# A hybrid decoder layer on one core: the prompts' scores as plain fp32 matmuls of two key heads side by side, in four visits for eight

## The chip, the cores and the metric

The kernel runs on one core of a Trainium2 chip. The metric is the device time of one execution in microseconds; for the kernel before it is 1594.37 us, the median of 3 runs (1593.99 to 1594.84). One further execution was profiled; all views of the trace are of that one.

## The reference

One decoder layer for 256 prompt tokens and 64 sample tokens (8 sequences of 8) that share the weights, model width 2048. What matters here is the attention of the prompt: 16 query heads in 4 groups, one key head of 64 features for each group, a window of 128 positions in blocks of 128 queries.

```python
xn = rms_norm(x, g_mix)
z = xn @ w_in                      # [B | C | h | q | k | v | gate_conv | gate_attn]
s = einsum('...qhgd,...shd->...hgqs', q, k) * HEAD_DIM ** -0.5
s = where(valid, s + bias, -inf)   # bias: a learned value by head and distance
p = exp(s - m) / (sum(exp(s - m)) + exp(sink - m))
o = einsum('...hgqs,...shd->...qhgd', p, v)
m = sigmoid(gate_c) * y_conv + sigmoid(gate_a) * (o @ w_attn_out)
h = x + m @ w_o
h = h + (silu(hn @ w_gate) * (hn @ w_up)) @ w_down     # hn = rms_norm(h, g_ffn)
```

The output is the norm of h, with new keys, values and convolution states.

## The kernel before

Features lie on partitions and all 320 tokens on the free axis. Every large product (`product`, L162 to L185) works on 256 output features: its weights come in tiles of 4 x 128 rows (`wraw`), which ScalarE (ACT) rounds to `whi` (L129) and VectorE (DVE) turns into the rest `wlo` (L130), both of type fp32r. One tile gives 24 matmuls of 320 columns (L176): each weight block three times, high by high, high by the input's low part, low by high. Sixteen input blocks make 4 tiles, so a product of this kind has 96 matmuls. `wraw` has 4 buffers, `whi` and `wlo` 3 each, so the splits may run three tiles ahead of TensorE (PE).

Behind each tile `product` calls `tick` (L144), which runs one step of a generator in `side_work`: the small work of attention is cut into such steps and laid between the tiles. Instructions are then put in order on each engine by a scheduler; `after` holds a step's work behind the last split and the last matmul. `pending` (L181) holds work that is done once behind the first tile of the following product.

The products come in this order: kv (L371), four pairs of q (`q`, heads' queries), then four rounds of C, H and B for the convolution, then the gates (`gc`, `ga`) with the convolution's and the attention's output (`yc`, `ya`), then `wo`, `fg`, `fu` and `dn`. During q the side work is `kv_work` (L784): the first norm, whose sum over partitions is two matmuls `prb` (L199), the turning of keys and values, and `keys_twice`. During the rounds of C, H and B it is `attention`: scores and softmax of the prompt, its values (`po`, L612), and the sample's attention (`pss`, L684, and `spo`, L748), the last three in plain fp32.

The scores before use the split form too. `keys_twice` (L773) writes `k2`: for each of the 4 key heads a tile of 128 rows, in which 64 rows hold the rounded keys and 64 the rest, in both orders. `q_out` (L805) scales a pair of query blocks (L808) and writes for each head pair two tiles `q2` of 128 rows, rounded queries on one half and the rest on the other (L812 on ACT, L813 on DVE); they lie in `at_t`, which takes the attention's result later. A unit is one key head and two of its four query heads; there are 8. For each unit `prompt_scores` (L537) issues 6 matmuls of 256 columns: for each of two heads two that add up for the second block of queries (L548) and one for the first block, which sees only its own 128 keys, both parts side by side (L551). `ps1` and `ps0` take a PSUM bank each, from a pool of 4 (`aux`). DVE then adds the bias, read backwards (L556, L559), takes the larger of the two halves for the second block (L557), and adds the second part for the first block (L560). `prompt_softmax`, `prompt_norm` and `prompt_turn` follow, each in a later step. `bias_load` (L527) is a transfer that POOL (GpSimd) issues, into one of two buffers.

A nudge (L193) is a single matmul of `xh` by `xl`, with contiguous columns, into an `aux` bank that nobody reads. There are four of them in the kernel before: in the kv product, twice in the sample's attention, and one of 128 columns in the first `fu` product.

The lines in question:

Of the kernel before, what the change touches and what calls it, by code (L numbers as in the profile page):

```python
# [8 lines left out]
F32 = mybir.dt.float32  # L9
F32R = mybir.dt.float32r  # L10
AF = mybir.ActivationFunctionType
# [5 lines left out]
TP, NB, TS = 256, 8, 8  # L17
T = TP + NB * TS
DC = 1024
NH, NKV, HD, GRP = 16, 4, 64, 4  # L20
DKV = NKV * HD
WIN = 128
# [5 lines left out]
P = 128  # L28
# [19 lines left out]
LEAD_X, LEAD_C, LEAD_A, LEAD_M, LEAD_F, LEAD_L = 16, 8, 8, 24, 40, 48  # L48
# [4 lines left out]
def hybrid_layer(ctx: ExitStack, tc: tile.TileContext, a: dict, o: list):  # L53
    nc = tc.nc
# [17 lines left out]
    def ps_aux(name):  # L72
        return aux[0].tile([P, 512], F32, tag="aux", name=name)
# [3 lines left out]
    def u(s):  # L77
        uid[0] += 1
        return f"{s}_{uid[0]}"
# [10 lines left out]
    def tmp(tag, name):  # L90
        return wk.tile([P, UL], F32, tag=tag, name=u(name))
# [101 lines left out]
    def nudge(rows, weights, n):  # L193
        x, w = (bass.AP(r.tensor, r.offset, [list(r.ap[0]), [1, m]]) for r, m in ((rows(0), n), (weights(0), P)))
        nc.tensor.matmul(ps_aux(u("nudge"))[:, :n], w, x, start=True, stop=True)
# [5 lines left out]
    def flip(ap):  # L201

        *rest, (step, n) = ap.ap
        return bass.AP(ap.tensor, ap.offset + (n - 1) * step, [*rest, (-step, n)])
# [15 lines left out]
    rbq = cst.tile([P, T], F32, name="rbq")  # L220
# [31 lines left out]
    xh, xl = row_tiles(xp, ("xh_t", "xl_t"), KC, LEAD_X, ("xh", "xl"))  # L252
# [21 lines left out]
    kT = zz.tile([P, 2, T], F32, name="kT")  # L274
# [188 lines left out]
    at_row = 2 * NS * JS + JS  # L463
    at_t = yy.tile([P, LEAD_A + 8 * at_row + 16], F32R, name="at_t")
# [7 lines left out]
    pr = pr_p.enter_context(tc.tile_pool(name="pr", bufs=1, side="right"))  # L472

    k2 = pr.tile([P, NKV, 2, TP], F32R, name="k2")
    k2h, k2l = k2[:, :, 0], k2[:, :, 1]

    def q2(ch, par):
        o = LEAD_A + ch * at_row + par * TP  # L480
        return at_t[:, o:o + TP]


    def kv_turn(t):

# [41 lines left out]
    def bias_load(kv, gp):  # L527
        bias = pr.tile([P, 2, 2 * WIN], F32, tag="bias", name=u("bias"), bufs=2)
        nc.gpsimd.dma_start(
            bias,  # L530
            bass.AP(
                e_scr.tensor, e_scr.offset + (kv * GRP + gp * 2) * EL, [[1, P], [EL, 2], [1, 2 * WIN]]
            ),
        )
        return bias

    def prompt_scores(kv, gp, bias):  # L537

        j, par = kv // 2, kv % 2
        s = pr.tile([P, 4, WIN], F32, tag="s", name=u("s"), bufs=3)
        ps1, ps0 = ps_aux(u("ps1")), ps_aux(u("ps0"))
        for gi in range(2):
            q = q2(j * 4 + gp * 2 + gi, par)
            for i in range(2):
                nc.tensor.matmul(  # L548
                    ps1[:, gi * 256:(gi + 1) * 256], q[:, WIN:2 * WIN], k2[:, kv, i], start=i == 0, stop=i == 1
                )  # L550
            nc.tensor.matmul(  # L551
                ps0[:, gi * 256:(gi + 1) * 256].rearrange("p (two k) -> p two k", two=2), q[:, 0:WIN],
                k2[:, kv, :, 0:WIN], start=True, stop=True,
            )
        w = pr.tile([P, 2, 2 * WIN], F32, tag="w", name=u("w"), bufs=1)
        nc.vector.tensor_add(w, ps1.rearrange("p (g k) -> p g k", g=2), flip(bias))  # L556
        nc.vector.tensor_max(s[:, 2:4], w[:, :, 0:WIN], w[:, :, WIN:2 * WIN])  # L557
        p0 = ps0.rearrange("p (g two k) -> p g two k", g=2, two=2)
        nc.vector.tensor_add(s[:, 0:2], p0[:, :, 0], flip(bias[:, :, 0:WIN]))  # L559
        nc.vector.tensor_add(s[:, 0:2], p0[:, :, 1], s[:, 0:2])  # L560
        return s

    def prompt_softmax(kv, gp, s):
        h0 = kv * GRP + gp * 2
        mx = wk.tile([P, 2, 2], F32, tag="mx", name=u("mx"))
        den = wk.tile([P, 2, 2], F32, tag="den", name=u("den"))
        es = wk.tile([P, 2, 2], F32, tag="es", name=u("es"))
        nc.vector.tensor_reduce(mx.rearrange("p b g -> p (b g)"), s, axis=AX.X, op=ALU.max)
        nc.vector.scalar_tensor_tensor(
            mx, mx, -1.0, nsink[:, h0:h0 + 2].unsqueeze(1).to_broadcast([P, 2, 2]),  # L570
            op0=ALU.mult, op1=ALU.min,
        )
        nc.vector.tensor_add(es, sink_bc[:, h0:h0 + 2].unsqueeze(1).to_broadcast([P, 2, 2]), mx)
        for n in range(4):
            b, g = n // 2, n % 2
            nc.scalar.activation(
                s[:, n], s[:, n], AF.Exp, bias=mx[:, b, g:g + 1], accum_out=den[:, b, g:g + 1]
            )
        nc.scalar.activation(es, es, AF.Exp)
        return den, es  # L580
# [44 lines left out]
    units = [(j * 2 + par, gp) for j in range(2) for gp in range(2) for par in range(2)]  # L625

    def prompt_weights(scrs):
        bias, sc, sm = {}, {}, {}
        bias[0] = bias_load(*units[0])
        for i in range(len(units) + 1):  # L630
            if i < len(units):
                if i + 1 < len(units):
                    bias[i + 1] = bias_load(*units[i + 1])
                sc[i] = prompt_scores(*units[i], bias.pop(i))
                yield
                sm[i] = prompt_softmax(*units[i], sc[i])
            yield
            if i >= 1:
                prompt_norm(sc[i - 1], *sm.pop(i - 1))
                scrs.append(prompt_turn(sc.pop(i - 1)))  # L640
# [129 lines left out]
                        nc.gpsimd.tensor_copy(dst, src.bitcast(F32))  # L770
            yield

    def keys_twice():  # L773
        for kv in range(NKV):
            j, r0 = kv // 2, kv % 2 * 64
            src = kT[r0:r0 + 64, j, 0:TP]
            for o0 in (r0, 64 - r0):
                nc.scalar.activation(k2h[o0:o0 + 64, kv, :], src, AF.Copy)
            for o0 in (r0, 64 - r0):
                nc.vector.tensor_sub(k2l[o0:o0 + 64, kv, :], src, k2h[r0:r0 + 64, kv, :].bitcast(F32))  # L780
            yield

    def kv_work():
        yield from first_norm()  # L784
        rows = []
        for t in range(3):
            rows.append(kv_turn(t))
            yield
        yield from keys_twice()
        for t in range(3):  # L790
            kv_natural(t, rows[t])
            yield
# [11 lines left out]
    def q_out(j, gp, ps):  # L804
        for c in range(2):  # L805
            g = gp * 2 + c
            t = tmp("ta", "qt")[:, :TP]
            nc.vector.tensor_mul(t, ps[c][:, :TP], rbq[:, :TP])  # L808
            for par in range(2):
                r0, o0 = par * 64, 64 - par * 64  # L810
                q = q2(j * 4 + g, par)
                nc.scalar.activation(q[r0:r0 + 64], t[r0:r0 + 64], AF.Copy)  # L812
                nc.vector.tensor_sub(q[o0:o0 + 64], t[r0:r0 + 64], q[r0:r0 + 64].bitcast(F32))  # L813
            nc.vector.tensor_mul(
                qs[:, j, :, g * TS:(g + 1) * TS], ps[c][:, TP:T].rearrange("p (b t) -> p b t", b=NB),
                rbq[:, TP:T].rearrange("p (b t) -> p b t", b=NB),
            )

    side_work[0] = kv_work()
    for j in range(2):  # L820
        for gp in range(2):
            ps = in_pair(O_Q + (j * 2 + gp) * CW, "q")
# [4 lines left out]
    for cp in range(4):  # L827
        c_sb = []
        ps = in_pair(O_C + cp * CW, "C")
        for c in range(2):  # L830
            t = tmp("ta", "csb")
            nc.vector.tensor_mul(t[:, :T], ps[c][:, :T], rbsq)
            c_sb.append(t)
        ps = in_pair(O_H + cp * CW, "H")
        conv = []
        for c in range(2):
            ch = cp * 2 + c
# [12 lines left out]
            n = UL - 2  # L850
# [10 lines left out]
        ps = in_pair(O_B + cp * CW, "B")  # L861
        for c in range(2):
            ch = cp * 2 + c
            cv, cs = conv[c]
            t = tmp("td", "bc")
# [23 lines left out]
    for mp in range(8):  # L889
        c0 = mp * CW  # L890
        sg = {}
        for nm, off, tag in (("gc", O_GC, "ta"), ("ga", O_GA, "tb")):
            ps = in_pair(off + c0, nm)
            for c in range(2):
                t = tmp(tag, nm)[:, :T]
# [3 lines left out]
        ps = product(  # L899
            lambda k0, n: load_cols(w_co, k0, n, c0), 8,  # L900
            cv_h, cv_l, "yc",
        )
        for c in range(2):
            nc.vector.tensor_mul(sg["gc", c], ps[c][:, :T], sg["gc", c])
        ps = product(
            lambda k0, n: load_cols(w_ao, k0, n, c0), 8, at_h, at_l, "ya",
        )
        for c in range(2):
            t = sg["ga", c]
# [10 lines left out]
    for mp in range(8):  # L920
        c0 = mp * CW
        ps = product(
            lambda k0, n: load_cols(w_o, k0, n, c0), KC,
            m_h, m_l, "wo",
        )
        for c in range(2):
            k = mp * 2 + c
# [8 lines left out]
            else:  # L936
                t = tmp("tc", "sq")[:, :T]
# [126 lines left out]
    for half in range(2):  # L1064
# [7 lines left out]
        for fpair in range(nf // 2):  # L1072
# [11 lines left out]
            for c in range(2):  # L1084
                t, t2 = tmp("ta", "gs")[:, :T], tmp("tb", "sg")[:, :T]
# [94 lines left out]
    ps = [ps_acc(u("dn")) for _ in range(4)]  # L1180
    sets = [(k, k + 1) for k in range(0, nf, 2)]
    sets[-2:] = [sets[-2] + sets[-1]]
    for i, ks in enumerate(sets):
# [4 lines left out]
        for k, c, m in passes(order, end):  # L1188
            cs = slice(c * P, (c + 1) * P)
            if m == 0:  # L1190
                nc.tensor.matmul(
                    turns(placed(ps[c])[:, :, JR:]), held[k][0][:, cs], turns(a_move(k)[:, :, JR:]),
                    start=k == 0, stop=k == nf - 1,
                )
            elif m == 2:
                last["mm"] = nc.tensor.matmul(
                    turns(placed(ps[c])[:, :, 0:JT]), held[k][1][:, cs], turns(a_move(k)[:, :, 0:JT]),
                    start=False, stop=k == nf - 1, skip_group_check=True,
# [4 lines left out]
    s3, h3, v, s, r = (op.tile([P, 1], F32, name=n) for n in ("s3", "h3", "vf", "sf", "rr"))  # L1203
# [4 lines left out]
    for c in range(4):  # L1208
        k = E0 // P + c
# [11 lines left out]
    for c in (2, 3):  # L1221
        k = E0 // P + c
        first, _ = h_parts(k)
# [114 lines left out]
```

## Time and profile before

| | |
|---|---|
| median of 3 runs | 1594.37 us |
| the profiled execution | 1594.48 us |
| its span, first to last instruction | 1592.8 us |
| mean granted TensorE clock | 0.998 |
| the 8 visits of the scores | 90.6 to 143.3 us |
| PE, DVE, ACT busy from 98 to 113 us | 15.00, 14.29, 8.32 of 15.00 us |
| PE, DVE, ACT busy from 113 to 128 us | 15.00, 14.87, 8.08 of 15.00 us |

The span is what the profiler saw between the first and the last instruction, 1.7 us less than the execution's own time. PE are the matmuls; PEld are the loads of weights, which run beside them. Busy times of matmuls overlap, since they are pipelined: 301 ns is the length of one of 320 columns, while the next starts after some 140 ns. The chain of work that ended last gives start, length and what, so that a run of equal matmuls divided by their count is the pace. In groups of instructions, the numbers behind the bar are busy us, mean ns of one, then the idle time before them and what ended it. In a table by stretches the columns are PE, PEld, DVE, ACT and POOL, each with its number of instructions, then the granted clock, the DMA share and GB/s.

### The profile page before, as it was taken

The page shows a single profiled execution, that of the slowest core. Times are in us where ns is not written, and L with a number is a line of the kernel's source. Part 1 is how long each engine was busy: PE and PEld are TensorE (multiplying, and loading weights), DVE is VectorE, ACT ScalarE, POOL GpSimd, SP SyncE. Part 2 cuts the span into 40 slices and gives each one's busy share as a digit, 9 for nine tenths or more (in the row PEclk, how much of TensorE's full clock was granted, in tenths as well). Part 3 has the DMA queues.
Part 4 walks back from the last instruction along what each step waited for, and adds up shares of the span by engine and source line. Part 5 has one row for each costly group of instructions (what it writes and reads, how often), then busy time and mean ns, then how long its engine had stood idle before and what let it go on. Part 6 is the DMA issues. An engine that isn't in the chain of part 4 may idle for free.

```text
span 1592.8 us, 27120 instructions
## 1 busy us (share of the span) xinstructions
PE 1584.2 (99%) x11296; PEld 1569.0 (99%) x11296; DVE 882.6 (55%) x1258; ACT 650.2 (41%) x901; POOL 125.3 (8%) x214
## 2 busy tenths in 40 slices
PE   9999999999999999999999999999999999999998
PEld 9999999999999999999999999999999999999887
DVE  7889765455444455565555555553444455555556
ACT  7555344333333333444333333333333343344443
POOL 2223342000000003320000000000000000000000
PEclk9999999999999999999999999999999999999999
DMA  8666666444444444444444444455555544445652
GB/s 274 205 188 194 214 188 217 156 156 158 159 159 154 157 157 156 159 159 156 156 155 157 159 159 159 155 153 158 158 159 159 159 155 156 155 158 159 185 173 93
DMA packets 77090, 264.51 MB, mean 166 GB/s; under 512 B 9576, under 2 KB 13000, under 8 KB 76840
## 3 DMA queue, kind: packets, MB, share of 16 engines
q1 hardware_dynamic: 71880, 249.86, 49.3%
q0 software_dynamic: 4656, 12.25, 2.5%
q8 instruction: 88, 1.44, 0.4%
q10 hardware_dynamic: 432, 0.69, 0.1%
q14 instruction: 34, 0.28, 0.1%
HBM read 256.46 MB, written 8.26 MB: 166 GB/s over the span
## 4 chain that ended last, share of the span: by engine, by line
PE 99%; ACT 0%; DVE 0%; DVEq 0%; issue 0%
PE fu L176 19%; PE fg L176 19%; PE dn L1015 12%; PE wo L176 7%; PE ga L176 7%; PE gc L176 7%; PE q L176 3%; PE B L176 3%; PE H L176 3%; PE C L176 3%; PE ya L176 3%; PE yc L176 3%; PE dn L1040 3%; PE dn L1048 2%; PE kv L371 2%; PE dl L1044 1%
## 5 line engine op out<-in xcount | busy, mean ns | idle before, releaser
L130 DVE TENSOR_TENSOR wlo<-wraw,whi 128x1024 fp32r<-128x1024 f32 (+1 forms) x460 | 562.4, 1223 | 580.1 <-ACT whi L129 569.4
L129 ACT ACTIVATE whi<-wraw 128x1024 fp32r<-128x1024 f32 (+1 forms) x460 | 485.1, 1056 | 713.0 <-PE fu L176 131.9
L176 PE MATMUL fu<-hh_t,whi 128*128 128x320 f32 x704 | 205.1, 301 | 0.0
L176 PE MATMUL fu<-hl_t,whi 128*128 128x320 f32 x704 | 205.0, 301 | 0.0
L176 PE MATMUL fg<-hh_t,whi 128*128 128x320 f32 x704 | 205.0, 301 | 0.0
L176 PE MATMUL fg<-hl_t,whi 128*128 128x320 f32 x704 | 205.0, 301 | 0.0
L1015 PE MATMUL dn<-a_t,whi 128*128 128x320 f32 x896 | 162.6, 301 | 0.0
L176 PE MATMUL fu<-hh_t,wlo 128*128 128x320 f32 x704 | 158.8, 301 | 0.0
L176 PE MATMUL fg<-hh_t,wlo 128*128 128x320 f32 x704 | 158.8, 301 | 0.0
L1015 PEld LDWEIGHTS dn<-a_t,whi 128*128 128x128 f32 x896 | 137.5, 187 | 0.0
L176 PEld LDWEIGHTS fu<-hl_t,whi 128*128 128x128 f32 x704 | 131.7, 187 | 0.0
L176 PEld LDWEIGHTS fu<-hh_t,whi 128*128 128x128 f32 x704 | 131.6, 187 | 0.0
L176 PEld LDWEIGHTS fg<-hh_t,whi 128*128 128x128 f32 x704 | 131.6, 187 | 0.0
L176 PEld LDWEIGHTS fg<-hl_t,whi 128*128 128x128 f32 x704 | 131.6, 187 | 0.0
L176 PEld LDWEIGHTS fu<-hh_t,wlo 128*128 128x128 f32 x704 | 116.1, 187 | 0.0
L176 PEld LDWEIGHTS fg<-hh_t,wlo 128*128 128x128 f32 x704 | 116.1, 187 | 0.0
L1015 PE MATMUL dn<-a_t,wlo 128*128 128x320 f32 x448 | 103.9, 301 | 0.0
L1015 PEld LDWEIGHTS dn<-a_t,wlo 128*128 128x128 f32 x448 | 74.8, 187 | 0.0
L176 PE MATMUL gc<-xh_t,whi 128*128 128x320 f32 x256 | 74.5, 301 | 0.0
L176 PE MATMUL gc<-xl_t,whi 128*128 128x320 f32 x256 | 74.5, 301 | 0.0
L176 PE MATMUL ga<-xh_t,whi 128*128 128x320 f32 x256 | 74.5, 301 | 0.0
L176 PE MATMUL ga<-xl_t,whi 128*128 128x320 f32 x256 | 74.5, 301 | 0.0
(319 smaller groups left out, 2811.0 us busy)
## 6 DMA issues: line engine op xcount, KB each, us to landing
wraw<-in_w_in_dram SPq DMA_DIRECT2D x128, 512.0 KB, 3.7
wraw<-in_w_gate_dram SPq DMA_DIRECT2D x88, 512.0 KB, 3.6
wraw<-in_w_up_dram SPq DMA_DIRECT2D x88, 512.0 KB, 3.6
wraw<-in_w_down_dram SPq DMA_DIRECT2D x88, 512.0 KB, 3.6
wraw<-in_w_o_dram SPq DMA_DIRECT2D x32, 512.0 KB, 3.6
wraw<-in_w_conv_out_dram SPq DMA_DIRECT2D x16, 512.0 KB, 3.7
wraw<-in_w_attn_out_dram SPq DMA_DIRECT2D x16, 512.0 KB, 3.7
wraw<-in_w_kv_dram SPq DMA_DIRECT2D x6, 512.0 KB, 7.7
```

What stands on the lines that cost most here:

```text
L129: last["hi"] = nc.scalar.activation(hi, src, AF.Copy)
L130: last["lo"] = nc.vector.tensor_sub(lo, src, hi.bitcast(F32))
L176: last["mm"] = nc.tensor.matmul(turns(fives(ps[c][:, :T])), w[:, k, c * P:(c + 1) * P], turns(x(kc)), start=(kc == 0 and i == 0), stop=(kc ...
L371: last["mm"] = nc.tensor.matmul(turns(fives(ps[c][:, :T])), w[:, k, c * P:(c + 1) * P], turns(x(kc)), start=(kc == 0 and m == 0), stop=(kc ...
L1015: last["mm"] = nc.tensor.matmul(turns(fives(ps[c][:, :T])), parts[k][w][:, c * P:(c + 1) * P], turns(x(k)), start=k == 0 and m == 0, stop= ...
L1040: nc.tensor.matmul(turns(placed(ps[c])), parts[k][0][:, cs], turns(a_move(k)), start=k == 0, stop=False)
L1044: nc.tensor.matmul(low, a_low(k), parts[k][0], start=k == 0, stop=k == nf - 1)
L1048: last["mm"] = nc.tensor.matmul(turns(placed(ps[c])[:, :, 0:JT]), parts[k][1][:, cs], turns(a_move(k)[:, :, 0:JT]), start=False, stop=k == ...
```

## The change

The queries stay as they are, in one fp32 tile `qf` of 8 blocks, written by the one multiplication that scales them; `q2`, `k2` and `keys_twice` are gone, and with them 24 copies on ACT and 24 subtractions on DVE. The four steps of `keys_twice` stay as empty steps, with a nudge in the second.

A visit now serves two units, the two key heads that lie on rows 0 to 63 and 64 to 127 of a block of `kT`. For each of two query heads and each of two blocks of queries it issues two matmuls, one for each half of the rows: 64 rows of queries as weights, 128 or 256 columns of keys. There are 8 matmuls in a visit and 4 visits; each takes all 4 `aux` banks. The biased scores of the two units are made in the steps where they were made before (`prompt_biased`), with one addition less each. Two bias tiles are loaded ahead, and each further one after the addition that frees its buffer. A second nudge stands in the step behind the last visit.

```diff
-    k2 = pr.tile([P, NKV, 2, TP], F32R, name="k2")
-    k2h, k2l = k2[:, :, 0], k2[:, :, 1]
-
-    def q2(ch, par):
-        o = LEAD_A + ch * at_row + par * TP
-        return at_t[:, o:o + TP]
+    qf = pr.tile([P, 8, TP], F32, name="qf")
...
-    def prompt_scores(kv, gp, bias):
-        j, par = kv // 2, kv % 2
+    def prompt_scores(j, gp):
+        both = [(ps_aux(u("ps1")), ps_aux(u("ps0"))) for _ in range(2)]
+        for gi in range(2):
+            q = qf[:, j * 4 + gp * 2 + gi]
+            for b, n in ((0, WIN), (1, 2 * WIN)):
+                for par, (ps1, ps0) in enumerate(both):
+                    rows = slice(par * 64, par * 64 + 64)
+                    nc.tensor.matmul(
+                        (ps1 if b else ps0)[:, gi * n:(gi + 1) * n], q[rows, b * WIN:(b + 1) * WIN],
+                        kT[rows, j, 0:n], start=True, stop=True,
+                    )
+        return both
+
+    def prompt_biased(ps1, ps0, bias):
         s = pr.tile([P, 4, WIN], F32, tag="s", name=u("s"), bufs=3)
-        ps1, ps0 = ps_aux(u("ps1")), ps_aux(u("ps0"))
-        for gi in range(2):
-            q = q2(j * 4 + gp * 2 + gi, par)
-            for i in range(2):
-                nc.tensor.matmul(
-                    ps1[:, gi * 256:(gi + 1) * 256], q[:, WIN:2 * WIN], k2[:, kv, i], start=i == 0, stop=i == 1
-                )
-            nc.tensor.matmul(
-                ps0[:, gi * 256:(gi + 1) * 256].rearrange("p (two k) -> p two k", two=2), q[:, 0:WIN],
-                k2[:, kv, :, 0:WIN], start=True, stop=True,
-            )
         w = pr.tile([P, 2, 2 * WIN], F32, tag="w", name=u("w"), bufs=1)
         nc.vector.tensor_add(w, ps1.rearrange("p (g k) -> p g k", g=2), flip(bias))
         nc.vector.tensor_max(s[:, 2:4], w[:, :, 0:WIN], w[:, :, WIN:2 * WIN])
-        p0 = ps0.rearrange("p (g two k) -> p g two k", g=2, two=2)
-        nc.vector.tensor_add(s[:, 0:2], p0[:, :, 0], flip(bias[:, :, 0:WIN]))
-        nc.vector.tensor_add(s[:, 0:2], p0[:, :, 1], s[:, 0:2])
+        nc.vector.tensor_add(
+            s[:, 0:2], ps0[:, 0:2 * WIN].rearrange("p (g k) -> p g k", g=2), flip(bias[:, :, 0:WIN])
+        )
         return s
...
     def prompt_weights(scrs):
-        bias, sc, sm = {}, {}, {}
-        bias[0] = bias_load(*units[0])
+        bias, both, sc, sm = {}, {}, {}, {}
+        for i in range(2):
+            bias[i] = bias_load(*units[i])
         for i in range(len(units) + 1):
             if i < len(units):
-                if i + 1 < len(units):
-                    bias[i + 1] = bias_load(*units[i + 1])
-                sc[i] = prompt_scores(*units[i], bias.pop(i))
+                if i % 2 == 0:
+                    both[i], both[i + 1] = prompt_scores(units[i][0] // 2, units[i][1])
+                sc[i] = prompt_biased(*both.pop(i), bias.pop(i))
+                if i + 2 < len(units):
+                    bias[i + 2] = bias_load(*units[i + 2])
                 yield
+                if i == len(units) - 2:
+                    nudge(xh, xl, T)
                 sm[i] = prompt_softmax(*units[i], sc[i])
             yield
...
-        yield from keys_twice()
+        for i in range(4):
+            if i == 1:
+                nudge(xh, xl, T)
+            yield
...
-            t = tmp("ta", "qt")[:, :TP]
-            nc.vector.tensor_mul(t, ps[c][:, :TP], rbq[:, :TP])
-            for par in range(2):
-                r0, o0 = par * 64, 64 - par * 64
-                q = q2(j * 4 + g, par)
-                nc.scalar.activation(q[r0:r0 + 64], t[r0:r0 + 64], AF.Copy)
-                nc.vector.tensor_sub(q[o0:o0 + 64], t[r0:r0 + 64], q[r0:r0 + 64].bitcast(F32))
+            nc.vector.tensor_mul(qf[:, j * 4 + g], ps[c][:, :TP], rbq[:, :TP])
```

More of the change, by code (lines that the diff above doesn't have):

```diff
@@ L771, in sample_attention @@
             yield
[L773 to L781, printed above, removed]
     def kv_work():
```

## The prediction, made before the changed kernel ran

> **What bounds it now.** I read the page's engine totals first, then who makes PE wait, then the chain of work that ended last, in the two stretches that hold plain fp32 work or the scores.
>
> ```profile
> span 1592.8 us, 27120 instructions
> PE 1584.2 (99%) x11296; PEld 1569.0 (99%) x11296; DVE 882.6 (55%) x1258; ACT 650.2 (41%) x901; POOL 125.3 (8%) x214
> ```
>
> ```profile
> PE wm L304 <- PEq L1321: 0.8, 1, 0.8
> ```
>
> PE is busy 1584.2 of 1592.8 us, and the only wait that the list has for it is one of 0.8 us at the very start. So the time is the sum of what PE does; other engines count only where they would make it wait. The second view is the chain from the first normalization to the first visit of the scores (start, length, what).
>
> ```profile
> 39.27 0.29 PE prb L199 x2
> 39.55 47.79 PE q L176 x336
> 87.34 3.41 PE C L176 x24
> 90.75 0.24 PE ps L548 x2
> 90.99 0.12 PE ps L551
> 91.11 0.23 PE ps L548 x2
> 91.34 0.12 PE ps L551
> ```
>
> Two things are to be seen. A visit of the scores, six matmuls of 256 columns, takes 0.24 + 0.12 + 0.23 + 0.12 = 0.71 us, or 0.118 each. And the 336 matmuls of q take 47.79 / 336 = 0.1422 us each, the 24 of C behind them 3.41 / 24 = 0.1421. The third view is the chain further on, around the three places that already use plain fp32 (po, pss, spo) and two nudges.
>
> ```profile
> 197.25 5.33 PE po L612 x48
> 202.58 3.58 PE H L176 x24
> 206.16 10.08 PE B L176 x72
> 216.24 1.99 PE pss L684 x64
> 218.23 3.62 PE B L176 x24
> 221.85 0.14 PE nudge L195
> 221.99 13.45 PE C L176 x96
> ...
> 252.24 1.92 PE spo L748 x128
> 254.16 3.58 PE B L176 x24
> 257.75 0.15 PE nudge L195
> ```
>
> Here 96 matmuls of C take 13.45, 0.1401 each: the same matmul runs at two paces, 0.1422 and 0.1400, a difference of 0.0022. The slow pace holds from prb at 39 us to the first visit of the scores. It comes back after pss, where the 24 matmuls of B take 3.62, and goes with the nudge at 221.85.
>
> **The change part by part.** The first place is PE's order at the first visit; ps are the scores' sums, k is k2, at_t holds the split queries. Before:
>
> ```order
> L548 MATMUL ps_134_1188<-k_496,at_t 128x256 x2
> L551 MATMUL ps_135_1189<-k_496,at_t 128x256
> L548 MATMUL ps_134_1188<-k_496,at_t 128x256 x2
> L551 MATMUL ps_135_1189<-k_496,at_t 128x256
> L176 MATMUL C_1137<-xh_t,whi_1203 128x16x5x4
> ```
>
> Now, at the same place, with keys and queries as they are:
>
> ```order
> L539 MATMUL ps_127_1134<-kT,qf 128x128
> L539 MATMUL ps_129_1136<-kT,qf 128x128
> L539 MATMUL ps_126_1133<-kT,qf 128x256
> L539 MATMUL ps_128_1135<-kT,qf 128x256
> L539 MATMUL ps_127_1134<-kT,qf 128x128
> L539 MATMUL ps_129_1136<-kT,qf 128x128
> L539 MATMUL ps_126_1133<-kT,qf 128x256
> L539 MATMUL ps_128_1135<-kT,qf 128x256
> L176 MATMUL C_1093<-xh_t,whi_1154 128x16x5x4
> ```
>
> Eight visits of six matmuls become four of eight: four pairs, each pair one head on rows 0 to 63 and one on rows 64 to 127. The removed work is 8 x 0.71 = 5.68 us of PE. For the new work the nearest rows are the plain fp32 ones:
>
> ```profile
> L612 PE MATMUL po<-pT,vn x32: 379/379/430, 197.2 to 202.2; 128*64 128x256 f32 x32
> L684 PE MATMUL pss<-kf,qs x64: 276/276/300, 216.2 to 218.0; 64*32 64x136 f32 x64
> ```
>
> The program issues 24 matmuls at L612 and the page has 48 records, 32 at L684 and 64 records: two records for each. The records overlap: 48 of 379 ns lie in 5.33 us, 64 of 276 ns in 1.99. At L612 two neighbours share the array by columns; at L684 four do, two by rows and two by columns. So po is 24 groups of 256 columns, pss 16 groups of 136, spo (128 records, four side by side) 32 groups of 64. What each costs, with what it does to the 24 matmuls behind it, is its length plus theirs less 24 x 0.140 = 3.36: po 5.33 + 3.58 - 3.36 = 5.55, pss 1.99 + 3.62 - 3.36 = 2.25 (of which 24 x 0.0022 = 0.05 is slow pace, so 2.20), spo 1.92 + 3.58 - 3.36 = 2.14. Two of these give a price by column and a fixed one: (5.55 - 2.20) / (24 x 256 - 16 x 136) = 0.000844 us a column, and 5.55 - 6144 x 0.000844 = 0.36 us for going in and out. They give spo 2048 x 0.000844 + 0.36 = 2.09, where it took 2.14. A visit of the change, if its pairs run side by side, is 2 x 2 groups of 128 and 2 x 2 of 256 columns: 1536 x 0.000844 + 0.36 = 1.66 us. Four are 6.64, and the scores cost 6.64 - 5.68 = 0.96 us more. No row shows two tiles of 64 rows that both use all 128 columns. The bounds are the streaming with no fixed price, 4 x 1.30 - 5.68 = -0.48, and pairs one behind the other (the second rival, below); I take side by side, since L684 is the nearest row and half of its overlap is by rows. The Trainium skill, page "TensorEngine Tiling (Array Packing)", section "Tiling Modes", lists 64x128 as two tiles that operate independently; no run here shows that form.
>
> Two nudges of 320 columns are added. The rows of today's have 0.14 and 0.15, and C behind the first is 0.01 over: 0.16 each, 0.32 together.
>
> The first new nudge stands in the q products:
>
> ```order
> L176 MATMUL q_829<-xh_t,wlo_833 128x16x5x4
> L176 MATMUL q_828<-xh_t,wlo_833 128x16x5x4
> L176 MATMUL q_829<-xh_t,wlo_833 128x16x5x4
> L195 MATMUL nudge_864<-xh_t,xl_t 128x320
> L176 MATMUL q_828<-xh_t,whi_868 128x16x5x4
> ```
>
> It comes 168 matmuls behind prb, with 192 of the 360 slow ones still to run until the first visit. If it works as the one at 221.85 did, they gain 192 x 0.0022 = 0.43. The visits themselves are another matter: the old ones ended the slow pace. Of the fp32 blocks the one on 64 rows (pss) left the slow pace; the one on 128 rows (po) left the fast one, since the 72 of B that come 24 matmuls behind it took 10.08, 0.140 each; behind spo a nudge comes too soon to tell. I take pss, being nearest: three gaps of 96 matmuls between visits, and 24 up to the second nudge, 312 x 0.0022 = 0.70. The other end is 0.
>
> What leaves the other engines is free of charge:
>
> ```profile
> L813 DVE TENSOR_TENSOR at_t<-qt,at_t 64x256 fp32r<-64x256 f32 x16 | 6.7, 420 | 1.1 <-ACT at_t L812 0.7
> ...
> L780 DVE TENSOR_TENSOR k<-kT,k 64x256 fp32r<-64x256 f32 x8 | 3.3, 418 | 0.1
> L560 DVE TENSOR_TENSOR s<-ps,s 128x256 f32<-128x256 f32 x8 | 3.3, 416 | 0.0
> ```
>
> ```profile
> L812 ACT ACTIVATE at_t<-qt 64x256 fp32r<-64x256 f32 x16 | 6.6, 415 | 6.2 <-DVE qt L808 6.0
> ```
>
> DVE loses 6.7 + 3.3 + 3.3 = 13.3 us and ACT the copies that feed these, but PE waits for neither now, so nothing of it shortens the span.
>
> What moves on DVE is the order. Before, the six operations of one unit stood between two weight splits (L556 to L573). Now two units' worth stand there, behind the first visit; s, w, mx and es are the tiles of the biased scores and their maxima:
>
> ```order
> L548 TENSOR_TENSOR w_1224<-ps_128_1135,bias_1131 128x512
> L561 SCALAR_TENSOR_TENSOR mx_1182<-mx_1182,nsink 128x4
> L549 TENSOR_TENSOR s_1223<-w_1224 128x256
> L565 TENSOR_TENSOR es_1184<-sink_bc,mx_1182 128x4
> L560 TENSOR_REDUCE mx_1260<-s_1223 128x4
> L561 SCALAR_TENSOR_TENSOR mx_1260<-mx_1260,nsink 128x4
> L565 TENSOR_TENSOR es_1262<-sink_bc,mx_1260 128x4
> L130 TENSOR_TENSOR wlo_1280<-wraw_1277,whi_1279 128x1024
> ```
>
> The split behind them, wlo_1280, belongs to the fourth product tile after the visit.
>
> ```profile
> 92.50 0.68 DVE L556 TENSOR_TENSOR w<-ps,bias 128x512 f32<-128x512 f32 x1
> ...
> 95.44 1.23 DVE L130 TENSOR_TENSOR wlo<-wraw,whi 128x1024 fp32r<-128x1024 f32 x1
> ```
>
> ```profile
> 128.00:151.00 23.00, 23.00 (x169) 23.00 (x168) 22.35 (x58) 11.98 (x35) 9.50 (x17) 1.00 0.67 202
> ```
>
> One unit took 95.44 - 92.50 = 2.94; without the second addition 2.5, two 5.0, with the split 6.2. The tile's first use of it is three tiles of 3.36 and 8 matmuls later, 11.2 us after the visit: 5.0 us to spare if DVE is up to date. DVE was busy 22.35 of 23 us late in this stretch (fourth column), and two additions less in every 15 us are 0.83, so it gets slacker, not tighter. I book 0. On POOL the loads of bias tiles, which wait for the addition two units back as before, are re-sorted among the stores of p_scr, with the convolution's copies queued behind; only DVE's later work waits for these, and PE has no wait there today.
>
> The sum: 0.96 + 0.32 - 0.43 + 0.70 = +1.55 us. The profiled execution took 1594.48 us, 0.11 above the median of the runs, 1594.37; so 1596.0 for it, and 1595.9 for a median. If the visits leave the fast pace it is 1595.2; with no fixed price as well, 0.32 - 0.43 - 0.48 = -0.59, 1593.8. A measurement of this kernel can tell about 0.2%, 3.2 us, from no change; all of these lie within that.
>
> **The rivals.** The first: the weights' loads are not hidden, since a pair needs two loads of 128 columns for each pass. A price is in the short nudge:
>
> ```profile
> 711.86 0.06 PE nudge L195
> 711.92 10.14 PE fu L176 x72
> ```
>
> A matmul of 128 columns takes 0.06, and the 72 behind it 10.14 - 72 x 0.140 = 0.06 more: 0.12 together, where streaming would be half, so about 0.12 is what a load takes when nothing covers it; the scores' 0.118 for 256 columns says the same. If the two loads of a pair go one behind the other, each of 8 passes lasts at least 0.236: a visit 8 x 0.236 + 0.36 = 2.25, four 9.00, +3.32 for the scores, and with the other terms +3.91: 1598.3, slower by 0.24%. For it: nothing in the trace loads 128 columns for two row halves. Against: spo has four loads of 32 columns in 1.92 / 32 = 0.06, which is less than one load of 128 took. There is a stronger form, that a load waits for its own half's matmul: then a 256-column pass is 0.118 + 0.216 and a 128-column one 0.118 + 0.108, a visit 4 x 0.334 + 4 x 0.226 + 0.36 = 2.60, and the whole +5.3, 1599.7. The Trainium skill, "TensorE: Matmul & The Clock Gate", section "Part 3: Packing small matmuls", says that loads overlap matmuls in flight only when the row group differs. The trace speaks against that: 96 matmuls on the same 128 rows, each with a load, run at 0.140.
>
> The second: the halves do not run side by side at all. Sixteen passes, 8 of 0.216 and 8 of 0.118, and 0.36: 3.03 a visit, 12.1 for four, +6.4, with the other terms +7.0: 1601.4, slower by 0.44%. It decides if the array takes two tiles together only where their columns differ, as in po and spo; against it is pss, whose four neighbours have two row halves.
>
> The third, also slower: DVE's double burst makes PE wait at the fourth tile after a visit. It decides if DVE comes to a visit more than 5.0 us late; then up to the burst's growth, 2.5 us, is lost at each of the three later visits, 7.5 in all: 1603.4. The busy share says no.
>
> That the change gains over 0.2% would need more than half of the 5.68 us of scores to vanish, which no row offers.
>
> **How the numbers follow.** Side by side with loads hidden, either pace: 0.80, all within 0.2%. Loads exposed: 0.08 (its weak form 0.06, its strong one 0.02). Halves in turn: 0.06. DVE's burst: 0.04. Gain: 0.02. The three cases before the gain are slower by over 0.2%, 0.18 in sum. The time is that of the likeliest case, 1595.9. The range reaches down to 1593.4 (1593.8 and half a microsecond of scatter, as the three runs of before lie 0.85 apart) and up to 1598.5, which takes in the weak form of the first rival.
>
> **What would show it.** In the changed kernel's chain: visits of about 1.66 us at four places (2.25, 2.60 or 3.03 for the rivals); a short group of q after a nudge near 63 us, then q at 0.140; the 96 matmuls between visits at 13.6 (slow) or 13.44 plus the way out; no PE wait between 90 and 155 us. I would be wrong if visits took over 2 us, if a wait of PE for wlo appeared, or if the slow pace outlived the second nudge.

## The result and the profile after

The changed kernel took 1596.91 us (median of 22 runs, 1595.96 to 1597.66), the kernel before beside it 1594.22 (median of 22; one of these runs took 4207 us, and the ratio leaves it out). The ratio is 1.0016, 95% interval 1.0010 to 1.0022: slower by 1.6 to 3.5 us, which is about the 0.2% that I had called the bound of no change. Forecast were 1595.9 us and a place between 1593.4 and 1598.5. So sign and range held, and 1.0 us of the size was missing. The profiled execution took 1597.15 us, 2.67 more than the profiled one before. First its totals:

```profile
span 1595.4 us, 27101 instructions
PE 1587.1 (99%) x11314; PEld 1569.5 (98%) x11314; DVE 871.0 (55%) x1226; ACT 640.3 (40%) x877; POOL 124.1 (8%) x214
```

PE is busy for 2.9 us more, DVE for 11.6 us and ACT for 9.9 us less. The span grew by 2.6 us, so the relief of DVE and ACT bought nothing, as expected. Where the 2.6 us lie shows in the chain that ended last (start, length, what), from the first normalization's sum to the tile behind pss:

```profile
39.24 0.29 PE prb L199 x2
39.53 23.89 PE q L176 x168
63.42 0.15 PE nudge L195
63.56 23.52 PE q L176 x168
...
90.44 1.51 PE ps L539 x16
91.95 10.28 PE C L176 x72
...
105.59 1.51 PE ps L539 x16
107.10 10.30 PE H L176 x72
...
137.45 3.58 PE C L176 x24
141.03 0.34 PE nudge L195
141.38 6.72 PE C L176 x48
148.10 14.00 PE H L176 x96
162.09 13.65 PE B L176 x96
...
199.64 5.33 PE po L604 x48
...
218.83 1.99 PE pss L681 x64
220.82 3.58 PE B L176 x24
```

In the chain before, the matmuls behind a visit and from 147 us on lost nothing (48 x 0.140 = 6.72, 96 x 0.140 = 13.44):

```profile
91.45 6.72 PE C L176 x48
...
146.85 13.44 PE H L176 x96
160.29 13.44 PE B L176 x96
```

Four things are to be read from the chain after, each as a length against a count times 0.140.

- **Visits.** One takes 1.51 us, and the 72 matmuls behind it 10.28 where 72 x 0.140 = 10.08 would do: with the 10.30 behind the next two that is 1.51 + 0.22 = 1.73. Four are 6.92, and the scores cost 6.92 - 5.68 = 1.24 us more than before.
- **First nudge.** The 168 matmuls of q ahead of it run at 23.89 / 168 = 0.1422, those behind at 0.140: 0.42 us won for 0.15.
- **Second nudge.** It takes 0.34 us instead of 0.15, and the 96 matmuls of H that follow a little later 14.00, where 96 x 0.1422 = 13.65 would do: 0.35 lost. PE waits here.
- **Slow pace.** From 148 us on, 0.1422 again: 13.65 / 96. It lasts through po and ends only at pss, behind which 24 matmuls take 3.58. That is 456 matmuls x 0.0022 = 1.0 us, less 0.05, since before B was slow behind pss and is not now.

The sum: 1.24 + 0.15 - 0.42 + 0.34 + 0.35 + 0.95 = 2.61 us, all of the span's 2.6. The prediction had 1.55, and no wait.

The matmuls of the visits, by source line (durations shortest / median / longest, first and last start, shapes):

```profile
L539 PE MATMUL ps<-kT,qf x64: 269/375/378, 90.4 to 137.1; 64*128 64x128 f32 x32, 64*128 64x256 f32 x32
```

Sixteen records in a visit, two for each of the 8 matmuls, as in po. The starts of the records stand in pairs, 6 ns apart, and behind the first pair it is from one pair to the next about 0.11 us for 128 columns and 0.216 for 256. Eight of the one and eight of the other, one by one, would be 2.6 us; they are done in 1.51 us. So the two halves do run side by side.

The waits from 130 to 155 us (who waited for whom: us in total, times, longest):

```profile
ACT s L568 <- DVE mx L561: 7.5, 2, 6.6
DVE wlo L130 <- ACT whi L129: 3.8, 2, 3.0
...
PEld H L176 <- ACT whi L129: 0.2, 1, 0.2
PEld nudge L195 <- DVE s L550: 0.2, 1, 0.2
```

The list of PE's own waits has nothing here, before or after; waits for data stand under PEld, the loads. They wait twice for 0.2 us, once in front of the nudge for DVE, which has to free a PSUM bank (L550 reads it), and once at the first H tile for ACT's rounded weights (whi). The long wait is above these: ACT stood for 6.6 us before the exponentials of the last visit, because DVE had not made their maxima. DVE's operations at this place, in order of time:

```profile
137.84 0.88 DVE L578 TENSOR_SCALAR s<-s,den 128x128 f32<-128x128 f32 x4
...
139.39 1.18 DVE L130 TENSOR_TENSOR wlo<-wraw,whi 128x1024 fp32r<-128x1024 f32 x1
140.49 0.41 DVE L550 TENSOR_TENSOR s<-ps,bias 128x256 f32<-128x256 f32 x1
...
148.03 1.23 DVE L130 TENSOR_TENSOR wlo<-wraw,whi 128x1024 fp32r<-128x1024 f32 x1 [2.97 <-ACT whi L129]
```

The visit ended at 137.45; DVE began its two units at 140.49, behind the previous unit's normalization and a weight split, 3.0 us late. Then ACT:

```profile
143.65 0.40 ACT L568 ACTIVATE s<-s,mx 128x128 f32<-128x128 f32 x1 [6.62 <-DVE mx L561]
...
146.95 2.94 ACT L129 ACTIVATE whi<-wraw 128x1024 fp32r<-128x1024 f32 x3
```

It takes the exponentials of both units in one go, from 143.65 to 146.95, and only then splits weights. The first of the three copies is done at 148.0, where PE could have begun its load some 0.2 us earlier. The DVE split behind it waits for ACT in turn (the 2.97 in brackets) and ends at 149.26, and here PE waits a second time, for wlo: its loads, 0.14 us apart as a rule, stand 0.30 apart at this place.

```profile
149.01 0.19 PEld L176 LDWEIGHTS H<-xl_t,whi 128*128 128x128 f32 x1
149.31 0.19 PEld L176 LDWEIGHTS H<-xh_t,wlo 128*128 128x128 f32 x1
```

The starts of the matmuls divide the tile's 0.35 us. At the wait for whi two steps take 0.258 and 0.247 us where 0.140 is the pace, 0.23 too much; at the wait for wlo two take 0.160 and 0.247, 0.13 too much. In both, the matmul behind the wait takes 0.247 us until the next one starts, so that a wait costs 0.11 us more than it lasts. The steps are 0.141 to 0.144 from the first H tile's second matmul on: the slow pace begins right behind the wait for whi.

### The profile page after: what moved, and what is told of

Read it like the earlier page. It is cut to its first block, busy times and chain, and to the rows that moved or that the text cites. A ratio compares the mean times of both kernels' runs of the same rounds, so it can differ in the third digit from the quotient of the medians.

```text
span 1595.4 us, 27101 instructions
## 1 busy us (share of the span) xinstructions
PE 1587.1 (99%) x11314; PEld 1569.5 (98%) x11314; DVE 871.0 (55%) x1226; ACT 640.3 (40%) x877; POOL 124.1 (8%) x214
## 4 chain that ended last, share of the span: by engine, by line
PE 99%; DVE 0%; ACT 0%; DVEq 0%; issue 0%
PE fu L176 19%; PE fg L176 19%; PE dn L999 12%; PE ga L176 7%; PE gc L176 7%; PE wo L176 7%; PE H L176 3%; PE B L176 3%; PE C L176 3%; PE q L176 3%; PE ya L176 3%; PE yc L176 3%; PE dn L1024 3%; PE kv L371 2%; PE dn L1032 2%; PE dl L1028 1%
## 5 line engine op out<-in xcount | busy, mean ns | idle before, releaser
L176 PE MATMUL wo<-m_h,whi 128*128 128x320 f32 x256 | 74.5, 301 | 0.0
L176 PE MATMUL wo<-m_l,whi 128*128 128x320 f32 x256 | 74.5, 301 | 0.0
```

The lines of the kernel that those rows point to most:

```text
L176: last["mm"] = nc.tensor.matmul(turns(fives(ps[c][:, :T])), w[:, k, c * P:(c + 1) * P], turns(x(kc)), start=(kc == 0 and i == 0), stop=(kc ...
```

## The experiments

My theory after the result: the two halves run side by side, and a visit costs streaming plus a fixed price for going into and out of the form with two row halves; the rest is the wait at the last visit and the pace that it leaves behind. The rivals: the halves overlap only in part, or the price is that of plain fp32 and not of the row halves; and the visits themselves, or the second nudge, set the pace. The kernels labelled e and b1 ran once each, beside one run of the kernel before at 1593.74 us; b2 and f1 ran in five rounds. Single runs of the changed kernel spread over 1.7 us, so I read the chains of the single ones and not their times.

**The halves in turn (e1).** All four matmuls of one half first, then the four of the other.

```diff
-        for gi in range(2):
-            q = qf[:, j * 4 + gp * 2 + gi]
-            for b, n in ((0, WIN), (1, 2 * WIN)):
-                for par, (ps1, ps0) in enumerate(both):
-                    rows = slice(par * 64, par * 64 + 64)
+        for par, (ps1, ps0) in enumerate(both):
+            rows = slice(par * 64, par * 64 + 64)
+            for gi in range(2):
+                q = qf[:, j * 4 + gp * 2 + gi]
+                for b, n in ((0, WIN), (1, 2 * WIN)):
```

> The four matmuls of the upper half of the rows stand in one row, then the four of the lower half, so that neighbours share their rows. If it is the alternation of the halves that lets two matmuls share the array, each visit's 16 passes go one after another: 8 x 0.216 + 8 x 0.11 = 2.6 us and 0.43 for going in and out, 3.0 us for 1.73, the span 5 us longer. If the hardware overlaps halves whatever their order, or if the overlap in the records is only pipelining, the visit stays at 1.7 and the span within 0.5 us.

It took 1598.09 us. The chain, and the matmuls of the second visit that are in flight from 106.51 to 106.78 us:

```profile
105.87 2.27 PE ps L539 x16
108.14 10.29 PE H L176 x72
```

```profile
L539 PE MATMUL ps<-kT,qf x5: 269/272/376, 106.3 to 106.8; 64*128 64x128 f32 x4, 64*128 64x256 f32 x1
```

A visit is 2.27 + 0.21 = 2.48 us, neither the 3.0 of halves in turn nor the 1.73 of halves side by side: both expectations missed. The second view tells why. In the order of the program one half has two records of 128 columns, then two of 256, then the same again, before the other half begins. Here, while the one of 256 that started at 106.3 is still in flight, four records of 128 columns start, and none of 256 between them: matmuls of the second half have started beside the first half's last ones, ahead of their turn (the starts are 106.558 and 106.564 us, the fifth record of one half and the first of the other). Four records of each half share their time, the others run alone, which leaves 2.6 less some 0.65 for streaming, and with the fixed price of 0.43 (below) 2.4. The first record of each half takes 0.21 us instead of 0.11, here twice in a visit and in the changed kernel once; that is about the 0.08 that remain. So the pairing by neighbours in the issue order is worth 0.75 us a visit, and the side-by-side reading of the changed kernel holds. The span grew by 1.0 us only, for this kernel has neither the wait at the H tile nor the slow pace behind it.

**All 128 rows (e2).** The same 8 matmuls, over the whole 128 rows.

```diff
-                    rows = slice(par * 64, par * 64 + 64)
+                    rows = slice(0, 128)
```

> Each of the 8 matmuls of a visit takes all 128 rows, so that both heads' features are summed: the scores are not the reference's. Nothing is side by side any more: streaming doubles, 1.30 to 2.6 us. If the fixed price of a visit (0.43 us: the first matmul 0.09 late, the first one behind it 0.20 late, the next few slower) is one of changing between 64 rows and 128, it goes, and a visit is 2.6; if it is one of plain fp32 beside fp32r, it stays, and a visit is 3.0. The span is 3.5 us longer in the first case, 5.2 in the second.

It took 1599.86 us. The chain:

```profile
107.17 2.62 PE ps L539 x16
109.79 10.09 PE H L176 x72
```

Sixteen records in a row, 2.62 us, just the streaming, and the 72 behind take 10.09: no price at the way out. So the fixed price of the changed visit is not one of plain fp32, but of going from the whole array to two tiles and back. It is not one of 64 rows alone: po divides the array by columns, on all 128 rows, and of its 5.33 + 0.22 us its 24 groups, 0.216 us apart, are 5.18, which leaves 0.37. The Trainium skill, "TensorEngine Tiling (Array Packing)", section "Tiling Modes", says that a change of the tiling mode drains the engine; the two rows above against the changed kernel's agree, and give it a size. They also answer the page that the prediction weighed, "TensorE: Matmul & The Clock Gate" of the Trainium skill, section "Part 3: Packing small matmuls", by which a load overlaps a matmul in flight only if the row group differs: here all loads are on the same 128 rows and none of them shows. What two tiles bring is 2.62 - 1.73 = 0.9 us a visit, since 0.43 of the 1.31 saved go for the change of form.

**Each matmul twice (e3).** To part the streaming from the fixed price.

```diff
-        for gi in range(2):
+        for gi in (0, 1, 0, 1):
```

> Each visit issues its 8 matmuls twice, with the same result. If a visit is 1.30 us of streaming and 0.43 of fixed price, it becomes 3.03 and the span 5.2 us longer, less what the second nudge and the tiles behind the last visit then need not wait. If more of it were fixed (loads at the start, a drain by matmul), the visit would grow by less than 1.0; if drains come with each pair, by more than 1.5.

It took 1601.71 us. The chain at the second visit:

```profile
106.88 2.82 PE ps L539 x32
109.70 10.44 PE H L176 x72
```

A visit is 2.82 where it was 1.51: 1.31 us for the second set of 1536 columns, 0.000853 a column. The prediction's 0.000844 stands. What is left of 1.73 is 0.42 to 0.43, the fixed price, where the prediction had 0.36 from po and pss; it is paid by the visit, not by the matmul. Behind two of the four visits the matmuls are slower than the 0.22 us explain (10.44 here): doubled visits do flip the pace at times, visits of 8 matmuls did so at none of 32 places in eight kernels.

**Without the second nudge (e4).**

```diff
-                if i == len(units) - 2:
-                    nudge(xh, xl, T)
```

> The second nudge is left out. Theory: the waits behind the last visit come from VectorE's double burst and ScalarE's exponentials behind it, which don't know of the nudge; PE comes to the H tile 0.34 us earlier and waits for its weights that much longer, the slow pace starts there all the same, and the span is within 0.2 us of the changed kernel's. Rival 1: the nudge itself brings the wait and the slow pace: without it neither is there, and the span is 0.34 + 0.35 + 1.0 = 1.7 us shorter. Rival 2: the nudge is plain added work: 0.34 shorter, the slow pace stays.

It took 1597.05 us, as much as the changed kernel. The chain:

```profile
137.50 8.35 PE C L176 x59
145.86 1.16 ACT s L568 x6
...
148.11 14.04 PE H L176 x96
162.15 13.65 PE B L176 x96
```

The H tile starts 12.12 us behind the start of the last visit, with the nudge it was 12.16, and the chain now runs through ACT's exponentials and its copy to whi. PE reaches the tile earlier by the nudge's 0.34 us and waits that much longer: nudge and wait fill one hole, which ends when whi is there. And the slow pace (13.65 / 96) is there without the nudge, so the nudge does not start it. By the starts of the matmuls it begins at the same tile, here behind the wait for wlo.

**The second nudge three tiles later (e5)**, behind the wait.

```diff
-                if i == len(units) - 2:
-                    nudge(xh, xl, T)
                 sm[i] = prompt_softmax(*units[i], sc[i])
             yield
+            if i == len(units):
+                nudge(xh, xl, T)
```

> The second nudge stands three tiles later, behind the tiles at which PE waited. If the slow pace begins with those waits and a nudge ends it, the matmuls from the nudge on, near 154 us, to the block po run at 0.140, where they ran at 0.142: 0.9 us less than the changed kernel, of which the longer wait at the H tile gives nothing back beyond what the earlier nudge cost. If the nudge only works by chance, or if the slow pace is a matter of where a product lies, the pace behind it stays 0.142 and the span the same.

It took 1596.7 us. The chain behind the wait:

```profile
148.23 7.15 PE H L176 x48
155.38 0.15 PE nudge L195
```

Of the 7.15, 48 x 0.140 = 6.72 is the fast pace; of the other 0.43, 0.27 lies between the starts of the matmuls, behind the two waits, and the rest in where the chain begins to count. This time the waits had left the pace fast, and there was nothing for the nudge to end. Inconclusive on its point; it does show that a wait need not bring the slow pace.

**DVE relieved (e6).** The normalization's four multiplications are left out, so DVE comes to each visit earlier.

```diff
-        for n in range(4):
-            nc.vector.tensor_scalar(s[:, n], s[:, n], den[:, n // 2, n % 2:n % 2 + 1], None, op0=ALU.mult)
```

> The four multiplications by which each unit's weights are normalized are left out (the output is not the reference's), 0.88 us of VectorE by unit, nothing else. Theory: VectorE then comes to the last visit up to 1 us or more earlier, the burst and the exponentials behind it end earlier, the second nudge and the H tile's weights wait for nothing, and the pace stays 0.140 from 141 us to the block po: 0.2 + 0.35 + 1.0 = about 1.5 us less. If the waits come from something else (the load of weights, the nudge's own bank, the visit), they stay at the same places, and the span changes by less than 0.3 us.

It took 1595.59 us. The chain at prb and from the last visit on:

```profile
39.29 0.29 PE prb L199 x2
...
141.08 0.15 PE nudge L195
141.23 6.74 PE C L176 x48
147.97 13.44 PE H L176 x96
...
198.37 5.33 PE po L602 x48
```

The nudge is back at 0.15, H takes 96 x 0.140 with no wait, and the pace stays fast. From prb to po it is 198.37 - 39.29 = 159.08 us against 199.64 - 39.24 = 160.40: 1.32 us less, where the nudge's 0.19, the wait's 0.35 and 360 x 0.0022 = 0.79 of pace make 1.33. The nudge's and H's lost time come from DVE's lateness; that is shown. The slow pace went with the waits, but a wait alone does not bring it, as e5 showed and the next one shows again.

**Without the first nudge (e7).**

```diff
-            if i == 1:
-                nudge(xh, xl, T)
```

> The first nudge is left out. The 360 matmuls from prb to the first visit then all run at 0.142: 0.43 us more, 0.15 less, so 0.28 longer in the chain up to 90 us. If the pace recovers by itself without a nudge, 0.15 shorter.

It took 1596.18 us. The chain of the four q products:

```profile
39.97 47.04 PE q L176 x336
```

47.04 / 336 = 0.140, without a nudge. The expectation of 0.142 missed: prb, which the prediction took to start the slow pace, ended one here. At the H tile behind the last visit this kernel waited for whi and wlo as the changed one does, and its pace stayed fast (the 96 of B behind it took 13.44). Five kernels have these waits: the changed one, e3, e4, e5 and e7. The pace behind them was slow in two, the changed one and e4.

**The first nudge in the kernel before**, once (b1) and then in five rounds (b2).

```diff
-        yield from keys_twice()
+        for i, _ in enumerate(keys_twice()):
+            if i == 0:
+                nudge(xh, xl, T)
+            yield
```

> The kernel before with nothing but a nudge in the q products, one tile earlier than the changed kernel's. If the nudge acts by itself, 216 matmuls run at 0.140 for 0.142: 0.48 less, 0.15 more, 0.33 us less in the chain up to 90 us, and the span 0.3 shorter than before. If it needs the changed kernel around it (no splitting of queries and keys), the pace stays and the span is 0.15 longer.

It took 1593.63 us. Here q ran at 0.140 from prb on, and the nudge had nothing to end.

> The kernel before with nothing but the nudge in the q products, timed. Where prb leaves a slow pace the nudge gains 0.48 and costs 0.15; where it doesn't it only costs 0.15. If both are about as common, 0.1 us less than before, which these rounds can't tell from nothing; if the slow pace is the rule, 0.33 less.

The median of 11 runs is 1593.97 us beside 1594.41, ratio 0.9997, interval 0.9988 to 1.0006: undecided. In its profiled execution the pace was slow, and the chain shows the gain where the nudge finds something to do:

```profile
39.52 20.48 PE q L176 x144
...
60.14 26.88 PE q L176 x192
```

0.1422 before it (20.48 / 144), 0.140 behind it (26.88 / 192): with the 24 of C, 216 x 0.0022 = 0.48 us for 0.15.

**The changed kernel without its wait (f1).** For three of the eight units, those that lie ahead of a visit, ACT does the normalization's multiplications; the second nudge goes.

```diff
+            by = den[:, n // 2, n % 2:n % 2 + 1]
+            if on_act:
+                nc.scalar.activation(s[:, n], s[:, n], AF.Copy, scale=by)
+            else:
+                nc.vector.tensor_scalar(s[:, n], s[:, n], by, None, op0=ALU.mult)
...
-                if i == len(units) - 2:
-                    nudge(xh, xl, T)
...
-                prompt_norm(sc[i - 1], *sm.pop(i - 1))
+                prompt_norm(sc[i - 1], *sm.pop(i - 1), on_act=i in (2, 4, 6))
```

> The changed kernel without its second nudge, and with the scaling of the units 1, 3 and 5 on ScalarE, which waits there, in place of VectorE: 0.88 us less of VectorE ahead of each later burst. Theory: no wait of PE behind the last visit, the pace stays 0.140 from the last visit to the block po, and the second nudge isn't missed: 0.34 + 0.35 less in every execution, 1.0 less in those whose waits began a slow pace, so 0.7 to 1.7 below the changed kernel, 1595.2 to 1596.2, still about 1 us above the kernel before: four visits of 1.73 for 5.68. Rival: the waits come from ScalarE's own queue, and 12 copies more on it make them longer: waits at the same place, no gain or a loss.

The median of 11 runs is 1595.5 us (1595.05 to 1596.02) beside 1594.41, ratio 1.0008, interval 0.9999 to 1.0017. The chain:

```profile
135.53 1.51 PE ps L539 x16
137.04 10.30 PE C L176 x72
147.34 13.44 PE H L176 x96
```

No wait, no slow pace up to pss, and the same visits of 1.51 + 0.22. This answers e6 with a kernel that computes everything: its span is 1593.3 us, 2.1 under the changed one, of which 168 x 0.0022 = 0.37 is chance: behind prb the pace was fast here, and the first half of q ran at it. What it still has over the kernel before is the price of the visits. Against the kernel before of the five rounds it is 1.1 us slower, and 1.24 for the visits and 0.15 for the first nudge, less some of the pace in q, is about that; its interval just reaches no change. Neither version is shown to beat the kernel before.

## Why the prediction was right, and where its steps were not

- **What bounds the kernel**: right. PE's 2.9 us more became 2.6 of span, and 21.5 us less on DVE and ACT became none.
- **Removed work, 5.68 us**: right by the accounting, which closes on the span's 2.6 us with it.
- **The visits, 1.66 each, +0.96**: the mechanism held, and the size was off. The price by column was right (0.000853 measured by doubling, 0.000844 forecast), the fixed one 0.43 instead of 0.36. I took it from po and pss, whose loads have 64 and 32 columns. By the starts of the records the first group behind the change of form takes 0.214 us in a visit where a later one takes 0.112, 0.10 more; in po 0.267 for 0.216, 0.05 more; in pss 0.140 for 0.116, 0.02 more. That goes with the 128, 64 and 32 columns of the loads, and the rest of the price is 0.31 to 0.32 in all three. So this is the part that was missing; that it is the first load, which nothing covers, is how I read it, and no experiment changed the loads alone. Cost: 1.24, not 0.96.
- **The nudges, 0.16 each**: right for the first (0.15), wrong for the second (0.34), which stood in front of a wait and took part of it. As e4 shows, it cost nothing net there.
- **Pace in q, -0.43**: right in this execution, -0.42. But in e7, f1 and others the pace behind prb is fast, so the gain is there only in some executions.
- **Slow pace behind the visits, +0.70 by the row of pss**: wrong place. Behind each visit of the changed kernel the pace was fast; pss was the wrong nearest row, and the other end, 0, was right. By luck a slow pace of +0.95 came from elsewhere in the profiled execution.
- **DVE's double burst, booked at 0**: this is the step that failed. I followed one thread: the split of wlo on DVE, with 5.0 us to spare until the fourth tile. DVE came 3.0 us late, inside that. But behind DVE's maxima stand ACT's exponentials of both units, 3.3 us in one piece, and behind those, in ACT's order, the copies of whi for the same tile. That second thread runs out first, and the split of wlo waits for it too. It cost 0.19 + 0.35 us, and then the slow pace in some executions. "No PE wait between 90 and 155 us" fell with it, and one of the signs that the prediction named for being wrong came: PE waited for wlo. A slow pace also stood behind the second nudge, but it began only there and had not outlived it. A busy share of 22.35 of 23 us on DVE was the warning, and I read from it only that less work makes it slacker.
- **The rivals.** Exposed loads (visits of 2.25 or 2.60): out, 1.73 was measured. Halves in turn (3.03): out; even when issued in turn they took 2.48. DVE's burst: its mechanism came true in small, at one visit of three, by some tenths instead of 2.5 us, and by way of ACT.

So the range held because the bounds were kept open, not because each term was right: the misses are +0.28 on the visits, +0.17 on the nudges, +0.35 on the H tile's wait, and +0.26 on the pace, in another place than forecast; 1.06 us in sum.

## What to carry to other kernels

When two tiles of 64 rows share the array, their gain has to pay for going into and out of that form, so many pairs belong in one visit; here 0.43 of the 1.31 us saved went for the change. When work is gathered into bursts, follow every engine's queue behind the burst to the first thing that PE needs, not only the engine that does the burst: the wait came through the second engine, whose own work was light. And relief on an engine is worth something only where PE waits for it: 21.5 us less on DVE and ACT bought nothing, while 0.88 us less of DVE for each unit took away the 0.54 us of the waits (e6).

## What the hardware did that I had not expected

The two paces of a 320-column matmul, 0.1400 and 0.1422 us, are not set by the kind of block in front of them alone. In the profiled executions of the twelve kernels here, the pace turned from fast to slow at prb in 6, from slow to fast in 5, and was fast before and behind it in one. At pss it turned from fast to slow in 11; in the changed kernel it turned from slow to fast. A nudge found the slow pace 33 times and ended it every time, and never started one. The waits of PE at the H tile were followed by the slow pace in two kernels of five. A block that simply swaps the paces would explain all of pss and all but one case of prb, but at po a slow pace stayed slow in the changed kernel and turned fast in e4, so what decides stays open. It is worth about 1 us here, where single runs of the changed kernel spread over 1.7.

The other surprise is in e1: matmuls of one row half started beside earlier ones of the other half, the first of them with the fifth of that half's eight records, though the program has it behind the eighth.
